# Alternating the solving product of one chunk with the inner product of the next in an RWKV-7 recurrence

## The chip, the cores and the metric

The kernel runs on one core of a Trainium2 chip. The metric is the time of one execution in device microseconds (us), here the median of several runs. A profile is one more execution, recorded by the hardware profiler; its times are counted from the first instruction.

## The reference, cut to what matters

The model is a decoder trunk of two layers over 16 meta tokens and 256 tokens of width 2048: RWKV-7 time mixing, a squared-ReLU MLP, gated linear attention, a second MLP, all in float32. The change lies in the first layer. With 32 heads of 64, the reference runs its recurrence token by token:

```python
    def step(S, inp):
        r_t, w_t, k_t, v_t, a_t, b_t = inp
        sa = jnp.einsum('bhvk,bhk->bhv', S, a_t)
        S = S * w_t[:, :, None, :] + sa[..., None] * b_t[:, :, None, :] + v_t[..., None] * k_t[:, :, None, :]
        y = jnp.einsum('bhvk,bhk->bhv', S, r_t)
        return S, y
```

Each head's output `y` is then normalised over its 64 values, gets a bonus term, is multiplied by a gate and goes through the output matrix `w_o`.

## The kernel before, in words

Activations lie transposed, features on the partitions, as 16 tiles of 128 x 272 tokens. Large products are made of float32r products: weights and operands are split into a high and a low part, and three products replace one (`mm3`, L156 to L162). A weight of 128 x 1024 is loaded by a DMA of SyncE's queue (SP) into one of three buffers `raw` (L131), cast to `hi` on ScalarE (ACT, L137) and subtracted to `lo` on VectorE (DVE, L138); of `hi` and `lo` there are two buffers.

The recurrence works on chunks of 64 tokens (five per head, the last with 16) and on 16 heads at a time: two groups `g`, each with chunks `c` from 0 to 4 (L892 to L970). Within a chunk the token-by-token update becomes a triangular system per head. Its inverse is worked out beforehand on DVE (`invert`, L539: 30 steps of two instructions, for two chunks and all 16 heads of a group at once). The system reaches DVE through DRAM (`scores`, L512, stores it with DMAs), and the inverse goes back through DRAM into the tile `AM` (L562). Because only 32 x 32 blocks are inverted so, `merge` (L636) completes a 64 x 64 inverse on TensorE in two rounds (L645, L655) of 32 x 32 products. There are four inversions and merges: number 2g for chunks 0 and 1 of group g, number 2g + 1 for the rest.

A chunk then has these steps on TensorE, each of 16 small float32 products, one per head, if nothing else is said. `AM` holds a chunk's matrices: partitions 0 to 63 multiply the values `v`, partitions 64 to 127 hold the inverse.

- `centre` (L663): eight products that transpose the values of a chunk and take out their mean; ACT copies them to the upper half of `uv` (L674, two copies). For the short chunk 4 GpSimd (POOL) clears `uv` first (L672).
- `inner` (L686): the values by the lower half of `AM`, into a bank of `pu`, called `ra`.
- `state` (L702): the state `S` by the keys, added to `ra` (L719), and by the receptances, into `pry` (L717): 32 products, taken in turn for the first part. Then `sides` (L695) negates `ra` into `rs` with two ACT instructions (L699). For chunk 0, which has no state, `inner` calls `sides` itself.
- `solve` (L722): the inverse by `rs`, into another bank of `pu` (L728); ACT copies the result to the second half of `uv` (L731).
- `carry` (L734): one product that puts `S` into a bank of `pu`, and `learn` (L739): keys by `uv` added to it; DVE scales the sum to the new `S` (L744).
- `emit` (L746): `uv` by the receptance half of `AM` (L752), the chunk's output; ACT copies it out (L754).
- `keys` (L676): eight transposes for the next chunk's `learn`.

The tag `pu` has two PSUM banks, given out in turn; `pm` (for centre and half of keys) has one.

The order on TensorE in this part is written out by hand (`manual_schedule`, L886). The other engines' queues get theirs from the scheduler, ordered by priority, weights far ahead. Between the small products stand *filling* units of large products: `R(n)` (L867) runs `n` units, `until(n)` (L872) runs on to unit number n, and a unit is three products of one weight column block. The 512 units are, in this order (L844): the value projection (units 0 to 255), then the output matrix in parts: 0 (256 to 287), 1 (288 to 319), A (320 to 383), 2 (384 to 447), 3 (448 to 511). An output part can begin only when the heads of its part are normalised (`norm`, L756) and split (L788). Eight units use up one weight. `some(it, n)` runs n steps of a generator, mostly of `invert`, whose instructions go to DVE. `GAPS` (L47) gives the units after `state` and after `solve` for each chunk; `MARK` (L49) gives the unit numbers that have to be reached before the four merges. In group 1 the scores for inversion 3 come first, with `R(3)` between them (L899).

At the very start, while the first activations are squared and summed, TensorE runs products without use (L361, L379) on a tile of ones, so that it is not idle.

Of the kernel before, what the change touches and what calls it, by code (L numbers as in the profile page):

```python
# [43 lines left out]

GAPS = [(4, 2), (4, 2), (4, 2), (4, 3), (5, 5)]  # L47

MARK = [120, 170, 244, 302]  # L49

OUTQ = [0, 1, 4, 5]
OUTA = [4, 5, 6, 7, 12, 13, 14, 15]
# [2 lines left out]
class Kern:  # L55
# [235 lines left out]
    def rwkv(self, done):  # L291
        nc, tc, ap = self.nc, self.tc, self.ap
# [23 lines left out]
        idle = self.pu()  # L316
# [42 lines left out]
        with tc.manual_schedule(engines={ENG.PE, ENG.DVE, ENG.Activation}):  # L359
            for _ in range(3):  # L360
                nc.tensor.matmul(idle, warm[:, :128], warm[:, :512], start=True, stop=True)  # L361
            for i in range(8):
                sq, h = self.t(ep, [P, 2, T], "x", KT), d[:, 2 * i : 2 * i + 2]
# [6 lines left out]
                for k in range(2 if i in (2, 5, 7) else 1):  # L370
                    nc.tensor.matmul(ss, warm[:, :128], sq[:, k], start=i == 0, stop=i == 7 and k == 1)
            w = warm.bitcast(F32R)
            v = w[:, :512]
            for x in (v.rearrange("p (a t) -> p t a", a=4), v.rearrange("p (a t c) -> p t a c", a=2, c=2),
                      v.rearrange("p (b a t) -> p b t a", a=2, t=16), v.rearrange("p (t a) -> p a t", a=2)):
                o = idle.rearrange("p (t a) -> p t a", a=x.shape[2]) if len(x.shape) == 3 else idle.rearrange(
                    "p (t a c) -> p t a c", a=x.shape[2], c=x.shape[3])
                for _ in range(3):
                    nc.tensor.matmul(o, w[:, :128], x, start=True, stop=True)  # L379
            om0 = self.one_minus(ep, "mix0")  # L380
            self.omka = self.one_minus(self.cp, "k_a")
            rstd = self.rstd_from(ep, ss, T, 1.0 / D, NORM_EPS, "kn", 2)
# [16 lines left out]
            def weight(kt):  # L399
                if kt:  # L400
                    raw = self.t(self.wp, [P, 1024], "raw", self.raw_bufs)
                    nc.sync.dma_start(raw, ap["w_r0"][kt])
                else:
                    raw = raw0
                return [raw] + [self.t(self.wp, [P, 1024], n, self.hi_bufs, F32R) for n in ("hi", "lo")]
# [9 lines left out]
            for kt in range(KT):  # L415
                w = weight(kt)
# [14 lines left out]
                p = parts.pop(0)  # L431
# [132 lines left out]
        for f in range(KT):  # L564
# [45 lines left out]
            if f == 13:  # L610
                inv = invert(0)
# [51 lines left out]
        def centre(g, c):  # L663
            full, n, nr = geom(c)[:3]
            pv = self.pm()
            for p in range(4):
                for e in range(2):
                    nc.tensor.matmul(pv[64 * e : 64 * e + nr, p * P : (p + 1) * P], hres[:, 8 * g + 4 * e + p, c * C : c * C + nr],
                                     self.cent, start=True, stop=True)
            x = uvs[g, c] = self.t(kp, [P, 16, 64], "uv", 2)  # L670
            if not full:
                nc.gpsimd.memset(x[0 : 2 * n], 0.0)  # L672
            for e in range(2):
                nc.scalar.copy(x[:nr, 8 * e : 8 * e + 8], pv[64 * e : 64 * e + nr].rearrange("p (h v) -> p h v", h=8))  # L674
# [11 lines left out]
        def inner(g, c):  # L686
            full, n, nr, am, lo, up, at = geom(c)
            uv = uvs[g, c]
            ra = ras[g, c] = bank(self.pu())
            for h in range(16):  # L690
                nc.tensor.matmul(ra[at[h % 2], h // 2], am[:n, h, :n], uv[:n, h], start=h < 2, stop=c == 0 and h > 13)
            if c == 0:
                sides(g, c)

# [7 lines left out]
        def state(g, c):  # L702
            full, n, nr, am, lo, up, at = geom(c)
            AR, ra = ARs[c > 1], ras[g, c]
            o = 128 * (c % 2) if full else 256
            ry = rys[g, c] = bank(self.pry())
            pq = [(p, q) for p in range(8) for q in range(2)]
            turns = [(*x, 0) for x in pq]
            outs = [(p, 1 - q, 1) for p, q in pq]
            if full:  # L710
                for i in range(7):
                    turns.insert(1 + 3 * i, outs.pop(0))

            for p, q, i in turns + outs:
                rows = slice(64 * q, 64 * q + 64)
                if i:
                    nc.tensor.matmul(ry[rows, p, :nr], sb[rows, p], AR[rows, p, o + n : o + n + nr], start=p == 0, stop=False)  # L717
                else:
                    nc.tensor.matmul(ra[at[q], p], AR[rows, p, o : o + n], sb[rows, p], start=False, stop=p == 7)  # L719
            sides(g, c)  # L720

        def solve(g, c):  # L722
            full, n, nr, am, lo, up, at = geom(c)
            uv, rs, pu = uvs[g, c], ras[g, c, "rs"], bank(self.pu())
            nu = n if full else 16
            for h in range(16):
                o = n * (1 - h % 2)
                nc.tensor.matmul(pu[o : o + nu, h // 2], am[up, h, :nu], rs[up, h], start=True, stop=True)  # L728
            for q in range(2):
                o = n * (1 - q)  # L730
                nc.scalar.copy(uv[n : n + nu, q::2], pu[o : o + nu])  # L731


        def carry(g, c):  # L734
            pS = pSs[g, c] = bank(self.pu())
            if c:
                nc.tensor.matmul(pS, self.ident, sb, start=True, stop=False)
# [129 lines left out]
        def R(n):  # L867
            for _ in range(n):
                if next(work, work) is not work:
                    ran[0] += 1  # L870

        def until(n):  # L872
            R(n - ran[0])

        def some(it, n):
            for _ in range(n):
                next(it, None)
# [8 lines left out]
        with tc.manual_schedule(engines={mybir.EngineType.PE}):  # L886
            R(43)
            for c, e in units1:
                some(inv, 5)
                R(13)  # L890
                scores(1, c, e)
            for g in range(2):  # L892
                last = nothing
                if g:

                    last = norm(0)
                    some(last, 1)
                    for c, e in units1:
                        R(3)  # L899
                        some(last, 1)  # L900
                        scores(3, c, e)
                    last = norm(1)
                until(MARK[2 * g])
                some(inv, 99)
                m = merge(2 * g)
                next(m)
                some(last, 1)
                R(4)
                next(m)
                inv = invert(2 * g + 1)  # L910
                some(inv, 3)
                until(128 + 128 * g)
                centre(g, 0)
                some(last, 1)
                R(2)
                keys(g, 0)
                some(last, 1)
                R(2)
                inner(g, 0)
                for _ in last:  # L920
                    R(4)
                    some(inv, 3)
                R(2)
                for c in range(5):
                    if c == 2:
                        R(8)
                        some(inv, 99)
                        if g == 0:
                            scores(2, 0, 0)
                        until(MARK[2 * g + 1])  # L930
                        m = merge(2 * g + 1)
                        next(m)
                        R(4)
                        next(m)
                        R(4)
                    if c:
                        state(g, c)
                    if g == 0 and c == 1:
                        fetch(2, ARs, ard)
                    if g == 0 and c == 2:  # L940
                        scores(2, 0, 1)
                    R(GAPS[c][0])
                    some(inv, 8)
                    solve(g, c)
                    if c < 4:
                        centre(g, c + 1)
                    if g == 0 and c == 2:
                        scores(2, 1, 0)
                    if c < 4:
                        carry(g, c)  # L950
                    R(GAPS[c][1])
                    some(inv, 8)

                    if c < 4:
                        learn(g, c)
                        inner(g, c + 1)
                    if g == 0 and c == 2:
                        scores(2, 1, 1)
                        inv = invert(2)
                    emit(g, c)  # L960
                    if c < 3:
                        keys(g, c + 1)
                    if g == 0:
                        if c == 0:
                            fetch(2, BKs, bkd)
                        if c == 2:
                            fetch(3, BKs, bkd)
                        if c == 4:
                            fetch(3, ARs, ard)
                    some(inv, 5)  # L970
            for g in (2, 3):
                for _ in norm(g):
                    R(2 * g)
# [298 lines left out]
```

## Time and profile before

| what | us |
|---|---|
| median of 3 runs | 2416.78 (2416.39 to 2419.48) |
| the profiled execution | 2421.71 |
| its span, first to last instruction | 2419.9 |
| TensorE busy in the span | 2371.1 |
| DVE busy | 1640.0 |
| ACT busy | 1242.5 |
| recurrence, about | 320 to 545 |

In a profile, PE is TensorE's products, PEld its weight loads, and `L728` line 728 of the kernel. A float32 product counts as two instructions. A row of the timeline reads: start, duration, engine, line, operation, output <- inputs, the tile and operand sizes, the count; in brackets the idle time before it and what ended that. A row of waits reads: total in us, number, longest. A product's duration contains its way through the array, so that rows overlap; what a group costs is seen from the start of one group to the start of the next.

### The profile page before, as it was taken

The numbers are of one execution on the slowest core, as the hardware profiler recorded it, in microseconds if no ns is written. First come the engines' busy times: TensorE is split into PE (matmuls) and PEld (weight loads), VectorE is DVE, ScalarE is ACT, GpSimd is POOL, SyncE is SP. The second block draws the span as 40 slices with busy tenths as digits, with TensorE's granted clock in tenths as the row PEclk, the third lists the DMA queues.
The fourth block names the chain that finished last, engine by engine and source line by source line (L and its number), as shares of the span: only waits on it lengthen the run. The fifth ranks groups of instructions, "written<-read, shape, count | busy, mean of one in ns | idle before, by whom it ended". The sixth has DMA issues, their size and how long they took to land. (4 is left out here: it accounts for less than half of the span.)

```text
span 2419.9 us, 47169 instructions
## 1 busy us (share of the span) xinstructions
PE 2371.1 (98%) x19262; PEld 2235.7 (92%) x19262; DVE 1640.0 (68%) x2748; ACT 1242.5 (51%) x1951; POOL 6.6 (0%) x20
## 2 busy tenths in 40 slices
PE   9999999899999999999999999999999999999998
PEld 8888888889999999999999999998999999999997
DVE  8777986858655555555556788778766666666666
ACT  6366544455555445345345555555555545445444
POOL 0000000000000000000000000000000000000000
PEclk9999999999999999999999999999999999999999
DMA  5578864524555555555555544445566666666665
GB/s 210 167 234 293 249 192 136 151 80 164 172 188 190 192 191 188 189 192 191 187 190 191 190 159 162 159 158 182 195 202 202 202 200 200 201 201 201 201 202 171
DMA packets 160729, 455.29 MB, mean 188 GB/s; under 512 B 34112, under 2 KB 50624, under 8 KB 160512
## 3 DMA queue, kind: packets, MB, share of 16 engines
q1 hardware_dynamic: 160512, 452.27, 57.4%
q8 instruction: 151, 2.47, 0.4%
q14 instruction: 66, 0.54, 0.1%
HBM read 433.86 MB, written 18.35 MB: 187 GB/s over the span
## 5 line engine op out<-in xcount | busy, mean ns | idle before, releaser
L137 ACT CAST hi<-raw 128x1024 fp32r<-128x1024 f32 (+1 forms) x818 | 794.3, 978 | 950.4 <-PE pj L161 524.8
L138 DVE TENSOR_TENSOR lo<-raw,hi 128x1024 fp32r<-128x1024 f32 (+1 forms) x818 | 926.2, 1139 | 512.1 <-ACT hi L137 503.5
L160 PE MATMUL pj<-x,hi 128*128 128x272 f32 x2240 | 640.7, 286 | 4.4 <-DVE hres L293 2.8
L162 PE MATMUL pj<-x,lo 128*128 128x272 f32 x2240 | 631.4, 282 | 5.8 <-DVE lo L138 5.6
L161 PE MATMUL pj<-x,hi 128*128 128x272 f32 x2240 | 628.2, 280 | 0.0
L189 PE MATMUL pj<-x,hi 128*128 128x512 f32 x1664 | 550.5, 384 | 3.8 <-ACT hi L137 3.0
L190 PE MATMUL pj<-x,lo 128*128 128x256 f32 x1664 | 457.0, 275 | 1.6 <-DVE lo L138 1.5
L160 PEld LDWEIGHTS pj<-x,hi 128*128 128x128 f32 x2240 | 424.3, 189 | 12.6 <-issue 4.7
L162 PEld LDWEIGHTS pj<-x,lo 128*128 128x128 f32 x2240 | 424.3, 189 | 10.7 <-DVE lo L138 9.6
L161 PEld LDWEIGHTS pj<-x,hi 128*128 128x128 f32 x2240 | 424.5, 190 | 3.2 <-issue 1.4
L189 PEld LDWEIGHTS pj<-x,hi 128*128 128x128 f32 x1664 | 315.3, 189 | 48.0 <-ACT hi L137 3.7
L189 PE MATMUL pj<-h,hi 128*128 128x512 f32 x1008 | 330.3, 382 | 0.0
L190 PEld LDWEIGHTS pj<-x,lo 128*128 128x128 f32 x1664 | 320.1, 192 | 4.6 <-DVE lo L138 4.1
L160 PE MATMUL pj<-h,hi 128*128 128x272 f32 (+1 forms) x1040 | 290.1, 279 | 0.0
L161 PE MATMUL pj<-h,hi 128*128 128x272 f32 (+1 forms) x1040 | 290.1, 279 | 0.0
L162 PE MATMUL pj<-h,lo 128*128 128x272 f32 (+1 forms) x1040 | 290.1, 279 | 0.0
L190 PE MATMUL pj<-h,lo 128*128 128x256 f32 x1008 | 274.8, 273 | 0.0
L189 PEld LDWEIGHTS pj<-h,hi 128*128 128x128 f32 x1008 | 190.5, 189 | 26.4
L160 PEld LDWEIGHTS pj<-h,hi 128*128 128x128 f32 x1040 | 196.6, 189 | 0.0
L161 PEld LDWEIGHTS pj<-h,hi 128*128 128x128 f32 x1040 | 196.6, 189 | 0.0
L162 PEld LDWEIGHTS pj<-h,lo 128*128 128x128 f32 x1040 | 196.6, 189 | 0.0
L190 PEld LDWEIGHTS pj<-h,lo 128*128 128x128 f32 x1008 | 193.5, 192 | 0.0
(268 smaller groups left out, 2115.4 us busy)
## 6 DMA issues: line engine op xcount, KB each, us to landing
raw<-mlp_w_d SPq DMA_DIRECT2D x512, 512.0 KB, 3.4
raw<-gla_in_d SPq DMA_DIRECT2D x98, 512.0 KB, 3.4
raw<-w_rkv_d SPq DMA_DIRECT2D x80, 512.0 KB, 4.0
raw<-gla_o_d SPq DMA_DIRECT2D x32, 512.0 KB, 3.4
raw<-rw_oQ_d SPq DMA_DIRECT2D x24, 512.0 KB, 3.3
raw<-w_r_d SPq DMA_DIRECT2D x16, 512.0 KB, 3.3
ard<-ar SPq DMA_DIRECT2D x16, 288.0 KB, 3.8
bkd<-bk SPq DMA_DIRECT2D x16, 288.0 KB, 3.9
```

The lines of the kernel that those rows point to most:

```text
L137: nc.scalar.copy(hi[:, h], raw[:, h])
L138: nc.vector.tensor_tensor(out=lo[:, h], in0=raw[:, h], in1=hi[:, h].bitcast(F32), op=ALU.subtract)
L160: nc.tensor.matmul(out, hi[:, ws], xh, start=first, stop=False)
L161: nc.tensor.matmul(out, hi[:, ws], xl, start=False, stop=False)
L162: nc.tensor.matmul(out, lo[:, ws], xh, start=False, stop=last)
L189: nc.tensor.matmul(wide, hi[:, ws], xt, start=kt == 0, stop=False)
L190: nc.tensor.matmul(one, lo[:, ws], xt[:, 0], start=False, stop=kt == nk - 1)
```

## The change

Six edits, all on the order of the instructions:

1. `inner` becomes a generator that stops after each product. `solve` gets a flag `beside`, and with it issues one product of the next chunk's `inner` after each of its own. It is set for chunks 0, 1 and 2. For chunk 3 `inner` of chunk 4 runs whole right after `solve`. Before, `inner` of the next chunk stood after `learn`.
2. `centre` of the next chunk moves from behind `solve` to ahead of the first filler.
3. `carry` moves from ahead of the second filler to behind it.
4. `GAPS` moves two units from ahead of `solve` to behind it, in chunks 0 to 3.
5. Two more units stand between the scores of inversion 3, and the marks for merges 1, 2 and 3 rise by 6, 22 and 26 units.
6. The last twelve products without use, in four access patterns, become thirteen in one.

```diff
-GAPS = [(4, 2), (4, 2), (4, 2), (4, 3), (5, 5)]
+GAPS = [(2, 4), (2, 4), (2, 4), (2, 5), (5, 5)]
-MARK = [120, 170, 244, 302]
+MARK = [120, 176, 266, 328]
...
-            v = w[:, :512]
-            for x in (v.rearrange("p (a t) -> p t a", a=4), v.rearrange("p (a t c) -> p t a c", a=2, c=2),
-                      v.rearrange("p (b a t) -> p b t a", a=2, t=16), v.rearrange("p (t a) -> p a t", a=2)):
...
-                for _ in range(3):
-                    nc.tensor.matmul(o, w[:, :128], x, start=True, stop=True)
+            x, o = self.weave(w[:, :512]), self.pairs(idle)
+            for _ in range(13):
+                nc.tensor.matmul(o, w[:, :128], x, start=True, stop=True)
...
             for h in range(16):
                 nc.tensor.matmul(ra[at[h % 2], h // 2], am[:n, h, :n], uv[:n, h], start=h < 2, stop=c == 0 and h > 13)
+                if h < 15:
+                    yield
...
-        def solve(g, c):
+        def solve(g, c, beside=False):
...
+            other = inner(g, c + 1) if beside else iter(())
             for h in range(16):
                 o = n * (1 - h % 2)
                 nc.tensor.matmul(pu[o : o + nu, h // 2], am[up, h, :nu], rs[up, h], start=True, stop=True)
+                next(other, None)
...
-                        R(3)
+                        R(5)
...
-                inner(g, 0)
+                some(inner(g, 0), 99)
...
+                    if c < 4:
+                        centre(g, c + 1)
...
                     R(GAPS[c][0])
                     some(inv, 8)
-                    solve(g, c)
-                    if c < 4:
-                        centre(g, c + 1)
+                    solve(g, c, c < 3)
+                    if c == 3:
+                        some(inner(g, 4), 99)
                     if g == 0 and c == 2:
                         scores(2, 1, 0)
+                    R(GAPS[c][1])
+                    some(inv, 8)
                     if c < 4:
                         carry(g, c)
-                    R(GAPS[c][1])
-                    some(inv, 8)
-
-                    if c < 4:
                         learn(g, c)
-                        inner(g, c + 1)
```

More of the change, by code (lines that the diff above doesn't have):

```diff
@@ L372, in rwkv @@
             w = warm.bitcast(F32R)
-            v = w[:, :512]
-            for x in (v.rearrange("p (a t) -> p t a", a=4), v.rearrange("p (a t c) -> p t a c", a=2, c=2),
-                      v.rearrange("p (b a t) -> p b t a", a=2, t=16), v.rearrange("p (t a) -> p a t", a=2)):
-                o = idle.rearrange("p (t a) -> p t a", a=x.shape[2]) if len(x.shape) == 3 else idle.rearrange(
-                    "p (t a c) -> p t a c", a=x.shape[2], c=x.shape[3])
-                for _ in range(3):
-                    nc.tensor.matmul(o, w[:, :128], x, start=True, stop=True)
+            x, o = self.weave(w[:, :512]), self.pairs(idle)
+            for _ in range(13):
+                nc.tensor.matmul(o, w[:, :128], x, start=True, stop=True)
             om0 = self.one_minus(ep, "mix0")
@@ L943, in rwkv @@
                     some(inv, 8)
-                    solve(g, c)
-                    if c < 4:
-                        centre(g, c + 1)
+                    solve(g, c, c < 3)
+                    if c == 3:
+                        some(inner(g, 4), 99)
                     if g == 0 and c == 2:
                         scores(2, 1, 0)
-                    if c < 4:
-                        carry(g, c)
                     R(GAPS[c][1])
@@ L954, in rwkv @@
                     if c < 4:
+                        carry(g, c)
                         learn(g, c)
-                        inner(g, c + 1)
                     if g == 0 and c == 2:
```

## The prediction

> **What bounds the kernel now.** I read the page first, then the summary of busy time by stretch for the recurrence (320 to 545 us), the list of waits of TensorE there, and last the timeline of single engines.
>
> ```profile
> span 2419.9 us, 47169 instructions
> PE 2371.1 (98%) x19262; PEld 2235.7 (92%) x19262; DVE 1640.0 (68%) x2748; ACT 1242.5 (51%) x1951; POOL 6.6 (0%) x20
> ```
>
> TensorE is busy for 98% of the span. So only TensorE work that becomes shorter, a TensorE wait that goes, or a better clock can pay. The change touches the start and the recurrence; there are few waits there:
>
> ```profile
> PE pt L655 <- DMA AM<-invd: 4.4, 2, 3.3
> PE pt L522 <- DVE AM L293: 2.3, 5, 1.0
> ```
>
> In the busy time by stretch, the first number after the stretch is its length, the next TensorE's busy time, and the number after POOL's the granted clock:
>
> ```profile
> 378.90:382.30 3.40, 2.27 (x72) 2.12 (x73) 0.00 (x0) 1.35 (x4) 0.00 (x0) 1.00 0.90 215
> 382.30:385.80 3.50, 3.50 (x70) 3.25 (x68) 1.65 (x3) 2.00 (x5) 0.00 (x0) 0.51 0.24 32
> ...
> 450.60:454.00 3.40, 1.05 (x10) 0.77 (x8) 2.09 (x4) 2.07 (x5) 0.27 (x1) 1.00 0.74 174
> 454.00:460.80 6.80, 5.84 (x79) 5.78 (x80) 0.82 (x4) 1.46 (x4) 0.16 (x1) 0.50 0.85 209
> 460.80:545.00 84.20, 83.04 (x1411) 74.67 (x1411) 51.58 (x125) 48.49 (x96) 0.94 (x1) 1.00 0.33 99
> ```
>
> The two waits of merge (L655) for the inverse's DMA lie in the first and third of these stretches, and after each the clock is half: for 3.5 us, and for 6.8 us.
>
> **The change, part by part.** The times of one chunk (group 0, chunk 1) carry most of the sum:
>
> ```profile
> 354.98 0.27 PE L719 MATMUL pu<-S,AR 64*64 64x64 f32 x1
> ...
> 355.90 0.22 PE L719 MATMUL pu<-S,AR 64*64 64x64 f32 x1
> 355.91 0.22 PE L717 MATMUL pry<-AR,S 64*64 64x64 f32 x1
> ...
> 356.47 0.38 PE L160 MATMUL pj<-x,hi 128*128 128x272 f32 x1
> ...
> 356.92 0.28 PE L160 MATMUL pj<-x,hi 128*128 128x272 f32 x1
> ...
> 358.06 1.15 PE L728 MATMUL pu<-rs,AM 64*64 64x64 f32 x32
> 359.14 1.09 PE L668 MATMUL pm<-cst,hres 128*64 128x128 f32 x16
> 360.16 1.13 PE L737 MATMUL pu<-S,cst 128*128 128x512 f32 x2
> ...
> 362.99 1.15 PE L691 MATMUL pu<-uv,AM 64*64 64x64 f32 x32
> ```
>
> *1. Solve and the next inner alternately, six times (two groups, chunks 0 to 2).* Now solve takes 1.08 us from its start to that of the next group (358.06 to 359.14), and inner, busy for the same 1.15, as long: 16 products each, two records a product. Within a group a product takes (1.15 - 0.22) / 16 = 0.058 us; some 0.15 is the change to the next group. Alternated, they read different halves of the rows (solve 64 to 127, inner 0 to 63) and write two banks. The nearest row is state, whose 32 products also go to two banks, partly in turn: 354.98 to 356.47, 1.49 us, where 32 x 0.058 + 0.15 = 2.01 would be serial. The middle rows show why: a product to pu and one to pry start 0.01 us apart. I take 1.49: 2.16 - 1.49 = 0.67 saved, six times **-4.0 us**. Ends: if all pairs run side by side, 16 x 0.058 + 0.21 = 1.14, so -6.1; if none does, 2.01, so -0.9. The low end has a row of its own: the scores alternate row halves and two banks as well, and are as slow as solve:
>
> ```profile
> 328.91 1.15 PE L522 MATMUL pt<-AR,BK 64*64 64x64 f32 x32
> ```
>
> The Trainium skill, TensorEngine Tiling (Array Packing), Key Properties, says of the tiles that they "operate independently: Different tiles can execute LdWeights and Matmul in parallel". By that the term would be the -6.1; the state row agrees in part, the scores row does not.
>
> *2. Centre moved ahead of solve, carry behind the second filler.* Centre's eight products (1.02 us) and carry's one (0.56) cost the same at either place. What moves with centre is ACT's work:
>
> ```profile
> 356.24 1.21 ACT L699 ACTIVATE rs<-pu 64x512 f32<-64x512 f32 x2 [0.46 <-PE pu L719]
> 358.05 1.14 ACT L137 CAST hi<-raw 128x512 fp32r<-128x512 f32 x2 [0.61 <-PE pj L161]
> 359.50 1.18 ACT L731 COPY uv<-pu 64x512 f32<-64x512 f32 x2
> 360.70 1.19 ACT L674 COPY uv<-pm 64x512 f32<-64x512 f32 x2
> ```
>
> The cover of sides (rs, 1.21 us) was four filler units; a unit is three products, 0.35 us (356.92 to 358.06 is three units and the turn to solve). It becomes centre (1.02) and two units (0.70), which is longer, so solve does not wait for sides. New is that the alternated inner needs centre's two uv copies. They start behind sides, at 357.5, and end at 358.7. TensorE arrives at 356.5 + 1.02 + 0.70 + 0.1 = 358.3 and needs the second copy eight pairs later. So the wait is about 0.1 at best, and 1.1 if the weight cast (1.14) gets in front of the copies. Queued behind a waiting inner product are all later TensorE products, the solve products among them. A weight is cast every eight units and a chunk has six; I let the cast hit one group of the six: +1.2, ends 0 and 6.6. Solve's own copies (1.18) then have four units (1.4) as cover before learn.
>
> Chunk 3 is not alternated, but its inner leaves the place between learn and state, where it hid the state's scaling on DVE:
>
> ```profile
> 408.20 0.68 DVE L293 TENSOR_TENSOR S<-pu,WC 128x512 f32<-128x512 f32 x1
> ```
>
> ```profile
> 409.29 1.08 PE L719 MATMUL pu<-S,AR 64*32 64x64 f32 x32
> ```
>
> State would now start 1.0 us sooner, at 408.3, and wait until 408.9; in chunks 0 to 2 keys still covers it. Twice 0.4: +0.8, ends 0 and 1.4. Chunk 4's POOL memset moves ahead with centre; it waits only for the emit two chunks back. New waits together **+2.0 us**.
>
> *3. Scores: five units instead of three between them.* TensorE waits there for DVE's masking of the scores before: five waits, 2.3 us. Ten units more give each 0.70 us, which takes all of four waits and most of the longest. DVE works in order and the inverse is in its queue, so I take **-1.5**, ends 0 and -2.3.
>
> *4. Merge of group 1 (mark 244 to 266).*
>
> ```profile
> 454.96 1.91 PE L655 MATMUL pt<-AM,rs 32*32 32x32 f32 x62 [3.28 <-DMA AM<-invd]
> ```
>
> Counted through the loops, the filler between the start of inverse 2 and this product grows from 64 to 80 units: 16 x 0.35 = 5.6 us. Less 1.5 of scores' waits, TensorE comes 4.1 us later against the inverse, and the wait is 3.28. The inverse's own chain ends in loads from SP's queue:
>
> ```profile
> 453.53 0.35 SPq L131 DMA_DIRECT2D raw<-rw_oQ_d x1
> 453.94 0.43 SPq L562 DMA_DIRECT2D AM<-invd x1
> ```
>
> Sixteen units bring two weights, each with one load on SP, two casts on ACT and two subtractions on DVE, but scores and normalisation are spread over a longer time, so DVE has no more to do before the inverse is done. The loads of the inverse stand in SP's queue behind weight loads (453.53 before 453.94), and two more weights go past them now. I take the wait as gone, -3.3, and with it the half clock: from 454.96 to 460.8 TensorE ran at half, 5.8 / 2 = -2.9. Together **-6.2**, ends 0 and -6.2.
>
> *5. Merge in group 0 (mark 170 to 176).* Of merge's 4.4 us of waits 1.1 are left for this one. Six units are 2.1 us, but two alternated groups before it bring TensorE 1.3 earlier, less waits of 0.4: net it comes 1.2 later. With full pairs (2.0 for 1.3) it comes 0.5 later. I take **-0.6** and no change of clock, ends 0 and -2.9 (1.1, and half of 3.5).
>
> *6. Warm-up: 13 products in one pattern for 12 in four.*
>
> ```profile
> 11.63 4.22 PE L379 MATMUL pu<-ar 128*128 128x512 f32 x12
> 15.67 0.42 PE L444 MATMUL pj<-x,hi 128*128 128x272 f32 x2
> ```
>
> ```profile
> 15.22 0.21 PEld L444 LDWEIGHTS pj<-x,hi 128*128 128x128 f32 x1 [0.24 <-ACT x L329]
> ```
>
> ```profile
> 1899.74 0.38 PE L189 MATMUL pj<-x,hi 128*128 128x512 f32 x1
> 1899.96 0.27 PE L190 MATMUL pj<-x,lo 128*128 128x256 f32 x1
> ```
>
> The twelve take 4.04 us and hold the first real product to 15.67, though its operand is there at 15.22. The nearest row for the new pattern, a product with 512 columns over alternating halves, takes 0.22 from start to start: 13 x 0.22 = 2.9. So at most 0.45 goes; I take **-0.2**. If the pattern were as slow as the last of the twelve (15.22 to 15.67), 13 x 0.45 would end 1.8 later.
>
> *7. Filling.* The units are the same in number: the last filling runs to 448 in both, so the 26 moved ahead of the last merge leave the end, where TensorE is full of the same products. I cost it at nothing. If products of layer output 2 (unit 384, now within the last normalisation) come before their operand is split, up to +1.5.
>
> Sum: -4.0 + 2.0 - 1.5 - 6.2 - 0.6 - 0.2 = -10.5. The profiled execution took 2421.7 us (1.8 around its span of 2419.9): 2411.2. The median is 2416.8, 4.9 less than it; carried over, **2406.3 us**.
>
> **The rivals.**
>
> *A: the alternation runs serially*, as the scores do, so the change doesn't do what it says. For it: the scores row. Against it: the state rows. The term is -0.9 instead of -4.0; TensorE comes later to merge 1, so 0.5 more of that wait goes: 2408.9 us.
>
> *B: merge 2 still waits*, for half its time, since the inverse's loads are queued behind more weights on SP, and the clock still falls: -1.6 instead of -6.2, 2410.9 us.
>
> *C: ACT casts a weight ahead of centre's copies every time.* Six waits of 1.1 and two of 0.7, 8.0 for 2.0: 2412.3 us. For it: the cast at 358.05 stands just there. Against: it was ready only when a weight was used up, once in eight units.
>
> *D, the other side: C and the clock.* The first stretch above holds a wait of 1.1 us and 2.27 busy of 3.40, and the next 3.5 us had half the clock. Six waits of 1.1 in the alternated groups, each followed by such a stretch, cost 6 x 1.7 = 10.2 on top of C: 2422.5 us. It decides from the third such stretch on (C leaves -4.5). Against it: the stretch from 460.8 kept clock 1.00 through many small products.
>
> The Trainium skill, TensorE: Matmul & The Clock Gate, HAM oscillation, warns of idle gaps over about 3.4 us only; by that D would stay at C's time. The trace does not agree: 1.1 us was enough once, though beside the 32x32 products.
>
> **How the numbers follow.** The forecast has 0.52, A 0.17, B 0.13, C 0.10, D 0.08. All best ends together (-6.1, 0, -2.3, -6.2, -2.9, -0.45) give 2398.8, but are not expected at once; A and C together give 2414.9. The range from 2400 to 2416 leaves out D and the extremes. About 0.2%, 4.8 us, is what a measurement of this kernel can tell from no change, so faster means under 2412.0: nearly all of the forecast and A, half of B, a little of C: 0.70. Within 0.2% is the rest of these, 0.20; slower is D and mishaps of its kind, 0.10.
>
> **What the profile after would show.** Step 1: L728 and L691 start 0.01 us apart, and the group takes 1.1 to 1.5 us; 2.0 is A. Step 2: TensorE's waits at L691 for uv of L674, none in sum over 2 us; at L719 for S in chunk 4. Steps 3 to 5: the L522 and L655 waits small, the clock 1.00 around the later merge. Step 6: L444 at about 15.3. The prediction is wrong if the clock falls elsewhere in the recurrence, or if the waits of L655 come back with the new marks.

## The result: 0.4% slower, and the profile after

| | median us (range, runs) | profiled execution | its span |
|---|---|---|---|
| before | 2419.01 (2416.39 to 2421.48, 6) | 2421.71 | 2419.9 |
| after | 2427.88 (2423.47 to 2434.41, 6) | 2423.47 | 2421.7 |

The ratio is 1.0041, with a 95% interval of 1.003 to 1.0051: slower by 8.9 us, where I forecast 10.5 us faster. The two profiled executions are only 1.8 us apart, since the one of before is longer than all six of its row and the one of after is the shortest of its six. So the traces show where the time goes, and the medians how much.

From the page of after, the head and the group of L160:

```profile
span 2421.7 us, 47169 instructions
PE 2362.8 (98%) x19263; PEld 2227.4 (92%) x19263; DVE 1640.1 (68%) x2748; ACT 1243.4 (51%) x1951; POOL 6.6 (0%) x20
...
L160 PE MATMUL pj<-x,hi 128*128 128x272 f32 x2240 | 639.5, 285 | 15.1 <-DVE hres L293 14.4
```

TensorE is busy for 8.3 us less than before (2371.1), and yet the kernel takes longer. The third row says why: 15.1 us of idle time ahead of L160, 14.4 of it on a DVE result in `hres`. L160 is filler; before, this group had 4.4. The waits of TensorE from 320 to 545 us (total, number, longest):

```profile
PE pj L160 <- DVE hres L293: 11.5, 2, 9.6
PE pj L162 <- DVE lo L138: 2.9, 2, 1.8
PE pu L717 <- DVE S L293: 2.4, 2, 2.0
PE pt L518 <- DVE AM L293: 2.0, 3, 1.3
```

Merge (L651 now) is no longer in the list: its waits of 4.4 us are gone. In their place stands one wait of 9.6 us in the filler ahead of merge 2. The timeline of TensorE there, only the rows of that wait and of the merge's two rounds:

```profile
460.94 0.57 PE L160 MATMUL pj<-x,hi 128*128 128x272 f32 x1 [9.64 <-DVE hres L293]
...
462.56 1.92 PE L641 MATMUL pt<-sysA,AM 32*32 32x32 f32 x64
...
467.43 1.76 PE L651 MATMUL pt<-AM,rs 32*32 32x32 f32 x58
```

The product waits for a bank of `pj`, and DVE frees it by adding the residual to it. DVE's timeline, its split of the outputs and that addition:

```profile
445.58 1.49 DVE L293 TENSOR_TENSOR x<-hres,x 128x272 fp32r<-128x272 f32 x4
...
460.35 0.82 DVE L293 TENSOR_TENSOR hres<-pj,hres 128x272 f32<-128x272 f32 x2 [7.19 <-DMA hres<-hT_d]
```

The split reads `hres` for the last time at 447.1; from then on the residual may be loaded into it. SP's queue:

```profile
445.34 3.31 SPq L131 DMA_DIRECT2D raw<-rw_oQ_d  x2
448.76 0.37 SPq L558 DMA_DIRECT2D AM<-invd  x1
450.14 0.33 SPq L131 DMA_DIRECT2D raw<-rw_oQ_d  x1
450.52 0.42 SPq L558 DMA_DIRECT2D AM<-invd  x1
453.19 0.33 SPq L131 DMA_DIRECT2D raw<-rw_oQ_d  x1
453.56 0.96 SPq L558 DMA_DIRECT2D AM<-invd  x2
454.57 1.91 SPq L831 DMA_DIRECT2D hres<-hT_d  x4
```

The residual (L831) stands behind weight loads and the inverse's pieces, and is issued at 454.57, 7.5 us after it could have been. It lands at 460.3. The weight loads ahead of it wait themselves: of SP's waits from 440 to 465 us the largest is that of L131 for `lo` (L138), 4.7 us in two, that is for a buffer `raw` to come free.

The same stretch by time; the columns are as in the prediction, the DMA engines' share is the next to last number:

```profile
445.00:451.30 6.30, 6.29 (x52) 5.88 (x51) 4.92 (x11) 2.96 (x7) 0.00 (x0) 1.00 0.58 185
451.30:460.90 9.60, 0.00 (x0) 0.00 (x0) 1.85 (x4) 1.05 (x2) 0.00 (x0) 0.69 0.90 215
460.90:475.40 14.50, 14.46 (x174) 12.84 (x175) 5.55 (x19) 4.99 (x12) 1.10 (x2) 0.50 0.01 4
475.40:545.00 69.60, 66.75 (x1249) 59.62 (x1247) 44.02 (x103) 39.41 (x76) 0.95 (x1) 1.00 0.38 111
```

Behind the wait, TensorE works through 14.5 us at half its clock, which costs another 7.2 us. Before, the stretch behind merge 2's wait had 6.8 us at half clock.

The clock accounts for about the whole loss. The mean granted clock of after's six runs is 0.9917; that of 31 runs of before (those beside E1 to E4) is 0.9968. Each run's time multiplied by its clock has a median of 2407.8 after and 2409.5 before (the clock is given to three digits, so one run is uncertain by 1.2 us); what is missing to the full time, the loss at half clock, grew from about 8 to about 20 us. This product counts a wait at half clock only half: in the trace of after 6.0 of the 9.6 us of waiting are at half clock, so some 3 of the 20 us belong to the wait. What TensorE has to do, waits among it, is then about as long as before.

### The profile page after: what moved, and what is told of

It is laid out like the page before. It is cut to its first block, busy times and chain, and to the rows that moved or that the text cites. A ratio compares the mean times of both kernels' runs of the same rounds, so it can differ in the third digit from the quotient of the medians.

```text
span 2421.7 us, 47169 instructions
## 1 busy us (share of the span) xinstructions
PE 2362.8 (98%) x19263; PEld 2227.4 (92%) x19263; DVE 1640.1 (68%) x2748; ACT 1243.4 (51%) x1951; POOL 6.6 (0%) x20
## 5 line engine op out<-in xcount | busy, mean ns | idle before, releaser
L138 DVE TENSOR_TENSOR lo<-raw,hi 128x1024 fp32r<-128x1024 f32 (+1 forms) x818 | 926.3, 1139 | 516.4 <-ACT hi L137 507.8
L160 PE MATMUL pj<-x,hi 128*128 128x272 f32 x2240 | 639.5, 285 | 15.1 <-DVE hres L293 14.4
L160 PEld LDWEIGHTS pj<-x,hi 128*128 128x128 f32 x2240 | 424.3, 189 | 23.4 <-issue 15.9
L160 PE MATMUL pj<-h,hi 128*128 128x272 f32 (+1 forms) x1040 | 290.1, 279 | 0.0
L160 PEld LDWEIGHTS pj<-h,hi 128*128 128x128 f32 x1040 | 196.6, 189 | 0.0
```

What stands on the lines that cost most here:

```text
L138: nc.vector.tensor_tensor(out=lo[:, h], in0=raw[:, h], in1=hi[:, h].bitcast(F32), op=ALU.subtract)
L160: nc.tensor.matmul(out, hi[:, ws], xh, start=first, stop=False)
```

## The experiments

"Before" here is the kernel before, run on the same chip; its median was 2415.9 to 2418.1. Clock is the mean granted clock of the runs. Each kernel has one trace, and the half clock differs between its executions (those of E16 took 2404.87 to 2414.53 us, at clocks from 0.999 to 0.996), so the stretches below show what happens in one execution, not its mean.

| kernel | median us (range, runs) | ratio to before [95%] | clock |
|---|---|---|---|
| E14 before, mark 266 | 2423.84 (2421.32 to 2428.33, 11) | 1.0025 [1.0017, 1.0034] | 0.9953 |
| E3 before, all filling edits | 2423.91 (2421.38 to 2431.79, 8) | 1.0029 [1.0017, 1.0042] | 0.9942 |
| E4 after, old filling and warm-up | 2416.98 (2413.40 to 2419.55, 11) | 0.9996 [0.9987, 1.0004] | 0.9961 |
| E1 after, parts on `r` first | 2420.74 (2414.77 to 2423.79, 11) | 1.0009 [1.0000, 1.0019] | 0.9950 |
| E2 after, mark 250 | 2420.70 (2416.64 to 2429.68, 12) | 1.0017 [1.0006, 1.0028] | 0.9938 |
| E7 after, residual on POOL's queue | 2421.27 (2415.03 to 2426.55, 12) | 1.0009 [0.9998, 1.0020] | 0.9951 |
| E8 E7, inverse steps issued later | 2420.71 (2418.09 to 2425.28, 11) | 1.0012 [1.0003, 1.0020] | 0.9947 |
| E9 E7, no alternation | 2422.25 (2417.05 to 2428.74, 12) | 1.0020 [1.0009, 1.0030] | 0.9942 |
| E10 E8, inverse's pieces on POOL too | 2412.63 (2406.35 to 2418.36, 12) | 0.9979 [0.9969, 0.9988] | 0.9958 |
| E11 before, both loads on POOL | 2411.12 (2408.57 to 2412.51, 6) | 0.9969 [0.9957, 0.9980] | 0.9980 |
| E12 E10, no alternation | 2414.12 (2409.08 to 2419.65, 11) | 0.9990 [0.9979, 1.0001] | 0.9956 |
| E13 E10, S covered | 2408.46 (2403.25 to 2413.25, 6) | 0.9955 [0.9939, 0.9972] | 0.9977 |
| E15 E4, both loads on POOL | 2408.91 (2407.05 to 2412.07, 7) | 0.9969 [0.9958, 0.9980] | 0.9971 |
| E16 E15, no alternation | 2408.94 (2404.87 to 2414.53, 9) | 0.9969 [0.9957, 0.9980] | 0.9978 |

The theory (W): the new mark lets output part 0 begin ahead of merge 2, its residual is late, and the wait takes the clock down. The rivals: the new order itself costs the clock (O), or the gains come out but are given back elsewhere (G).

### Does the filling alone make the loss?

**E14**, one number in the kernel before:

```diff
-MARK = [120, 170, 244, 302]
+MARK = [120, 170, 266, 302]
```

> The kernel before with one number changed: the mark of merge 2 is 266 instead of 244. Theory W (output part 0 stands ahead of merge 2 and waits for its residual): a wait of L160 for hres of 6 to 10 us, no wait of L655 over 1.5 there, at least 10 us at half clock behind it, 2420 to 2426 us. Rival P (the prediction's step 4: the wait of 3.3 for the inverse's pieces goes and nothing takes its place): 2411 to 2415 us.

Measured: 2423.84, 6.7 us slower. Its waits, and the stretch at half clock:

```profile
PE pj L160 <- DVE hres L293: 8.3, 1, 8.3
PE pt L522 <- DVE AM L293: 2.3, 5, 1.0
PE pt L655 <- DMA AM<-invd: 1.8, 1, 1.8
```

```profile
457.00:467.40 10.40, 6.14 (x82) 5.86 (x82) 2.10 (x8) 1.46 (x4) 1.10 (x2) 0.51 0.36 103
```

This is theory W. One number brings the wait (8.3 us), the half clock and most of the loss (6.7 of 8.9 us). Units 256 to 259 fill one bank of `pj` and 260 to 263 the other; unit 264 needs the first again. By this count a mark of 266 asks for it ahead of merge 2; and since four more units stand between the merge's two rounds, only a mark up to 260 would keep it behind them. No run tried a mark between 250 and 266. (The L655 wait of 1.8 us is that of merge 1, at 378.8; the clock stays full behind it.)

**E3**, all edits to the filling on the kernel before:

```diff
-MARK = [120, 170, 244, 302]
+MARK = [120, 176, 266, 328]
...
-                        R(3)
+                        R(5)
```

> The kernel before, with the filling moved alone: the new marks and five units between the scores, nothing else. W: the wait at unit 264 and the half clock are there, and nothing of the alternation's gain: 2428 to 2438 us. O: as the kernel before or a little faster, 2412 to 2420.

Measured: 2423.91, the same as E14, with a wait of 7.5 us for `hres` and 17.1 us at half clock beside it. The signs are those of W, but the time lies below its range (2428 to 2438) and above that of O. The other marks and the scores' spacing change nothing that can be seen beside it.

**E4**, the other half: the kernel after with the old marks, `R(3)` and the old warm-up.

```diff
-MARK = [120, 176, 266, 328]
+MARK = [120, 170, 244, 302]
...
-                        R(5)
+                        R(3)
```

> The changed kernel with the old marks, three units between the scores and the old warm-up: alternation, centre, carry and gaps alone. W: no wait at unit 264; the alternation saves about 1 us in each of six places: 2409 to 2415 us. O: slower than before, 2423 to 2430.

Measured: 2416.98, no different from before. So the order costs nothing, which speaks against O, but brings nothing either, where W said 2409 to 2415. Merge's two waits are as before (4.3 us in two). In this trace other waits of TensorE grew: for `lo` from 1.0 to 2.9 us, for `r` from 0.7 to 1.3, and there are new ones of 1.0 for centre's copy `uv` and of 0.9 for `S`, 4.4 us together, against six groups shorter by some 1.07.

### What if the wait is taken away?

**E1** puts the output parts that add into `r`, not `hres`, first; their loads are issued between 425 and 441 us. **E2** keeps merge 2 ahead of output part 0.

```diff
-OUTQ = [0, 1, 4, 5]
+OUTQ = [4, 5, 0, 1]
```

```diff
-MARK = [120, 176, 266, 328]
+MARK = [120, 176, 250, 328]
```

> The changed kernel, with output part 0 (and 1) taken in the order of columns 8-15 first (OUTQ 4, 5, 0, 1), so that the first additions use residuals that are loaded early. Theory W (the filling moved ahead of merge 2 starts output part 0 before its residual is loaded: a wait of 9.6 us at unit 264 and about 14.4 us at half clock after it, 7.2): the wait goes, the half clock with it, 10 to 17 us under the changed kernel, 2411 to 2418 us. Rival O (the new order around solve, with its own waits and small products, brings the clock down): the same as the changed kernel, 2425 to 2431.

> The changed kernel with the mark of merge 2 at 250 instead of 266, so that no unit of output part 0 runs ahead of it. W: the wait at unit 264 shrinks from 9.6 to 0 to 3 us, but a wait of 2 to 4 us for the inverse comes back at L651: 2413 to 2420 us. O: 2425 to 2431.

Measured: 2420.74 and 2420.70. The 9.6 us are gone in both, and the ratio falls from 1.0041 to 1.0009 and 1.0017, 6 to 8 us; but neither is faster than before, and both times lie between the ranges of W and O. W said that the half clock would go with the wait; it did not. E1's trace has four stretches of it, 20.5 us in all, each begun at or just behind a wait: for `S` (408.2), for a score's mask (442.4), at merge 2 (462.9) and for `r` (507.2). The waits of E1:

```profile
PE pt L651 <- DMA AM<-invd: 4.3, 1, 4.3
PE pj L160 <- DVE r L293: 2.9, 1, 2.9
PE pj L162 <- DVE lo L138: 2.9, 2, 1.8
PE pu L717 <- DVE S L293: 2.8, 1, 2.8
```

TensorE now comes to merge 2 before the inverse's pieces, and waits 4.3 us there, longer than before (3.3), in spite of the 80 units that I had counted as enough. The pieces pass SP's queue as well. The residual was the latest of two late loads.

**E7** leaves all as in after and loads the residual through POOL's queue, which is nearly empty (6.6 us busy).

```diff
                 if s == 0:
-                    nc.sync.dma_start(loc[f], ap["hT"][:, f])
+                    nc.gpsimd.dma_start(loc[f], ap["hT"][:, f])
```

> The kernel after, with the residual of the output parts (hres<-hT_d) loaded on POOL's queue instead of SP's. Theory W (the filler ahead of merge 2 waits for a residual that is late because it stands in SP's queue behind weight loads and the inverse's pieces; the 9.6 us of waiting and the 20.5 us at half clock that follow are the loss): the wait of L160 for hres goes below 1 us, TensorE reaches merge 2 some 9 us sooner and there waits 3 to 4.5 us for the inverse's pieces, as in the version with the parts reordered; half clock around it at most 7 us; 2414 to 2420 us. Rival P (POOL's own issue of a load is slow, or the load is late for what it must itself wait for): a wait of more than 4 us for hres stays, 2422 to 2430. Rival O (the new order with its short groups holds the clock down, whatever waits): the half clock between 400 and 480 us stays at 15 us or more, 2420 to 2426.

Measured: 2421.27, 1.3 above W's range and inside O's. The residual is no longer late: the split reads `hres` from 451.52 on, and the first residual is issued at 452.25.

```profile
451.52 1.49 DVE L293 TENSOR_TENSOR x<-hres,x 128x272 fp32r<-128x272 f32 x4
```

```profile
452.25 2.12 POOL L831 DMA_DIRECT2D hres<-hT_d  x4 [8.56 <-DVE x L293]
```

The wait for it ahead of merge 2 is gone, as W said. But the first two waits of TensorE are

```profile
PE pt L651 <- DMA AM<-invd: 4.9, 2, 4.6
PE pj L160 <- DVE hres L293: 2.9, 1, 2.9
```

(the second at 507.8, long after merge 2, where after has one of 1.9), and the longest of its three stretches at half clock lies elsewhere, ahead of them:

```profile
400.00:410.20 10.20, 8.14 (x186) 6.99 (x187) 5.51 (x18) 3.61 (x8) 0.15 (x1) 1.00 0.63 200
410.20:420.40 10.20, 10.20 (x91) 9.71 (x88) 7.13 (x18) 3.38 (x6) 0.00 (x0) 0.50 0.54 180
```

The first of these stretches holds the one wait for `S` (2.1 us); 10.2 us at half clock follow, and 6.8 more at merge 2: 17 us between 400 and 480 us, where W allowed 7 and O asked for 15. So W is right on the residual and wrong on the clock. O's reason, the short groups themselves, isn't needed for it: E9 below has none of them and 20.5 us at half clock, and E15, with the change's order on the old marks, has none from 320 to 545 us. What the order did bring is the longer wait for `S`.

**E10** takes the inverse's pieces off SP's queue too (and has the later inverse steps of E8, below):

```diff
-                    nc.sync.dma_start(x, invd[b][rows].rearrange("h s t -> s h t"))
+                    nc.gpsimd.dma_start(x, invd[b][rows].rearrange("h s t -> s h t"))
```

> As the kernel with the late inverse steps, and the inverse's pieces (AM<-invd) are loaded on POOL's queue too, so that they stand behind no weight load. Theory W: the waits of L651 go below 1 us in sum, the clock stays full around merge 2, 2408 to 2413 us: faster than both kernels. Rival M (the pieces were late for the inverse itself, not for the queue): the wait at merge 2 stays above 3 us, 2412 to 2418. Rival O: no wait, but half clock for 10 us or more between 400 and 480 us, 2414 to 2420.

Measured: 2412.63, the upper end of W, faster than both kernels. Half clock is left in two pieces of 3.4 us, at 408.9 and 439.6, behind waits for `S` and a score's mask. Two of its waits:

```profile
PE pj L160 <- DVE hres L293: 1.5, 1, 1.5
...
PE pt L651 <- DMA AM<-invd: 0.7, 1, 0.7
```

Rival M falls: merge 2 has no wait left to speak of, so the pieces were late for the queue.

**E11**: is it the change that then pays? The kernel before, with the same two lines changed:

> The kernel before, with the residual and the inverse's pieces loaded on POOL's queue, and nothing of the change. Theory Q (what the change could win in the merges is a matter of the queue alone): the waits of L655 fall from 4.4 to under 1.5 us, the half clock beside them goes, and the time is 2409 to 2413, no more than 1.5 above the changed kernel with both loads on POOL's queue. Rival D (the change pays once the queue is free, by its shorter groups): 2414 to 2417 us, at least 2 above that kernel.

Measured: 2411.12, theory Q. The waits of merge fall from 4.4 to 0.7, no stretch of the recurrence is at half clock, and the change adds nothing that can be told (E10: 2412.63).

```profile
PE pt L655 <- DMA AM<-invd: 0.7, 1, 0.7
```

```profile
435.00:470.00 35.00, 33.19 (x406) 30.59 (x406) 30.34 (x79) 20.54 (x47) 5.89 (x10) 1.00 0.62 171
```

What I had hoped to win in the merges by filling is won by the queue, without filling.

### The wait for S

**E8**: E7, with the steps of inverse 2 put behind the scaling of `S` in chunk 3 of group 0.

```diff
                     R(GAPS[c][0])
-                    some(inv, 8)
+                    if g or c != 3:
+                        some(inv, 8)
...
                     R(GAPS[c][1])
-                    some(inv, 8)
+                    late = g == 0 and c == 3
+                    if not late:
+                        some(inv, 8)
...
                         learn(g, c)
+                    if late:
+                        some(inv, 16)
...
-                    some(inv, 5)
+                    some(inv, 1 if g == 0 and c == 2 else 5)
```

> As the last, and in group 0 the DVE steps of inverse 2 that stood ahead of the scaling of S in chunk 3 are put behind it. Theory W: the wait of L717 for S falls from 2 to 2.8 us to under 0.8, the half clock that follows it in some runs goes with it; inverse 2 starts about as late as before, since it waits for its load anyway; 1.5 to 4 us less than the kernel with the residual on POOL's queue. Rival L (inverse 2 gets later by what S gains, and merge 2 waits for it): the same time as that kernel within 1 us, with the wait of L651 longer by 2 us or more.

Measured: 2420.71, the same as E7 ("the last" in the expectation). But the edit didn't do what it was for. DVE's queue is ordered by the scheduler, and the timeline of DVE shows inverse steps still ahead of `S`:

```profile
404.77 0.18 DVE L293 TENSOR_TENSOR upd<-sysA 64x30 f32<-64x30 f32 x1 [3.99 <-DMA sysA<-sysd]
...
407.11 0.68 DVE L293 TENSOR_TENSOR S<-pu,WC 128x512 f32<-128x512 f32 x1
```

DVE idles 3.99 us for the inverse's load, then runs nine instructions of the inverse, and only then scales `S`, whose sum is ready soon after 404. TensorE waits 2.7 us. Neither theory was tested by this run.

**E13** is E10 with that wait covered:

```diff
-MARK = [120, 176, 266, 328]
+MARK = [120, 176, 272, 328]
-OUTQ = [0, 1, 4, 5]
+OUTQ = [4, 5, 0, 1]
...
-                    if c == 3:
+                    if c == 3 and g:
                         some(inner(g, 4), 99)
...
                     emit(g, c)
+                    if c == 3 and not g:
+                        some(inner(g, 4), 99)
+                        R(6)
```

> The changed kernel with both loads on POOL's queue; in chunk 3 of group 0 inner(4) and six units are issued between emit and the next state, where TensorE waits up to 3.2 us for the scaling of S; the mark of merge 2 goes from 266 to 272, and the output parts on r go first. Theory S (that wait and its half clock are a loss of their own): no wait of L717 over 0.5 us, full clock from 400 to 430 us, 2407 to 2411 us. Rival G (merge 2 or the residual is bound by the inverse's and the norm's chains, which start no earlier): the waits of L651 and L160 grow by 2 to 3 us, and the time is within 1.5 us of the kernel without this edit, 2411 to 2414.

Measured: 2408.46, inside theory S, with no half clock in the recurrence. But the wait for `S` isn't under 0.5 us, it is 2.2 us in two from 400 us on, the longest 1.4; and the interval touches that of E10 (0.9969 to 0.9972 lies in both). That it beats before and after is shown; what each of its three edits brings isn't, nor that it beats E11, whose interval overlaps its own too.

### Does alternation reach the end?

**E9**, **E12** and **E16** are E7, E10 and E15 with each inner product whole behind solve:

```diff
-                    solve(g, c, c < 3)
-                    if c == 3:
-                        some(inner(g, 4), 99)
+                    solve(g, c)
+                    if c < 4:
+                        some(inner(g, c + 1), 99)
```

> As the kernel with the residual on POOL's queue, but every inner product is issued whole behind solve instead of alternately; all else stays. Theory W (each of the six alternated groups is 1.07 us shorter, and that reaches the end): 5 to 7 us more than the kernel with the residual on POOL's queue. Rival G (the gain is given back at the next wait for an inverse's pieces, for the scaling of S or for a score's mask): 0 to 3 us more, with these waits shorter here by as much.

> The changed kernel with both loads on POOL's queue and the late inverse steps, but every inner product is issued whole behind solve. The traces of the pair with the residual alone on that queue gave 1.84 us for the two groups one behind the other and 1.14 alternated. Theory W (with no wait for an inverse's pieces to give it back to, six times 0.70 reaches the end): 2415 to 2418 us, 3 to 5 more than the alternated one. Rival G (the gain is given back at the split of a weight on DVE and at the scaling of S): within 1.5 us of the alternated one.

**E15** is E4 with the two lines of POOL's queue.

> The order of the change alone (old marks, old units between the scores, old warm-up) with both loads on POOL's queue, so that neither the residual nor the inverse's pieces hold the merges. Theory W (the alternation's gain reaches the end when nothing gives it back and the clock stays full): 2406 to 2409 us, 2 to 5 below the kernel before with both loads on that queue (2411). Rival G (the gain is given back at the scaling of S, at a weight's split and at merge 2, which TensorE reaches earlier than its inverse is done): 2409.5 to 2413.

> As the last, but every inner product is issued whole behind solve. Theory W: 3 to 5 us more than the alternated one (six times 0.70). Rival G: within 1.5 us of it.

Measured, alternated and whole: 2421.27 and 2422.25, 2412.63 and 2414.12, 2408.91 and 2408.94. The timeline of TensorE in E9, from solve to the filler behind inner (354.13 to 355.97):

```profile
354.13 0.97 PE L727 MATMUL pu<-rs,AM 64*64 64x64 f32 x26
354.89 0.27 PE L687 MATMUL pu<-uv,AM 64*64 64x64 f32 x2
...
355.97 0.38 PE L160 MATMUL pj<-x,hi 128*128 128x272 f32 x1
```

One behind the other the two take 1.84 us: the first inner products start while solve runs. In E7 they take 1.14, so alternation itself is worth 0.70 a group, 4.2 in six. In the pair E7 and E9 the time from the start of merge 0 to that of merge 1 is nevertheless the same, 43.9 us (333.46 to 377.33 and 330.37 to 374.28): the filler between waits for a weight's split on DVE, in E7

```profile
371.41 0.38 PE L162 MATMUL pj<-x,lo 128*128 128x272 f32 x1 [1.83 <-DVE lo L138]
```

and in E9

```profile
368.36 0.38 PE L162 MATMUL pj<-x,lo 128*128 128x272 f32 x1 [0.44 <-DVE lo L138]
```

1.4 us, all that two groups gained. That is rival G, in this stretch of this pair; in the other pairs the same stretch is shorter with alternation, by 1.3 us (E10 and E12) and 0.6 (E15 and E16). Over the whole kernel the differences of the medians are 1.0, 1.5 and 0.0 us; the ratios to before differ by 0.11%, 0.11% and nothing, with intervals 0.1% to either side. Six times 0.70 did not come out in any pair. Whether 0 or 2 us reach the end stays open.

E15 lies in W's range in microseconds, 2.2 under E11. But before was 1.3 us faster beside E15 than beside E11, and the two ratios are the same, 0.9969: the order as a whole brings nothing that the medians can tell. The two traces do differ from the start of merge 0 to that of merge 3, E15 first:

```profile
333.35:492.75 159.40, 152.27 (x2548) 135.43 (x2547) 124.60 (x314) 87.14 (x176) 16.78 (x28) 1.00 0.51 149
```

```profile
334.67:497.25 162.58, 156.94 (x2548) 140.73 (x2547) 124.12 (x314) 87.26 (x176) 16.78 (x28) 1.00 0.50 145
```

At full clock the same 2548 instructions of TensorE take 3.2 us less in the new order. That is one execution of each; it points to a gain, and doesn't show one.

## Why the prediction was wrong, step by step

- **Step 1 (-4.0), mis-sized in the group, and not a gain at the end.** After, the pairs run side by side, at the better end that I gave:

```profile
488.35 0.27 PE L727 MATMUL pu<-rs,AM 64*64 64x64 f32 x1
488.35 0.27 PE L687 MATMUL pu<-uv,AM 64*64 64x64 f32 x1
...
489.44 0.38 PE L160 MATMUL pj<-x,hi 128*128 128x272 f32 x1
```

  1.09 us for both, where 2.16 stood before: 1.07 less, 6.4 in six. The value from the state row was too cautious. Rival A is out. Here the Trainium skill's sentence on independent tiles (TensorEngine Tiling (Array Packing), Key Properties) agrees with the trace. But I let the gain run to the end, and the experiments didn't find more than 2 us of it there.
- **Step 2 (+2.0), the sum right by chance.** No wait for centre's copies was left in after (I took 1.2; rival C is out). In E4 and E15, with the old marks, there is one, of 1.0 and 0.7 us: one group of six, as I took it. The wait for `S` is 2.4 instead of 0.8, nearly all of it in group 0:

```profile
407.79 1.08 PE L717 MATMUL pu<-S,AR 64*32 64x64 f32 x32 [2.05 <-DVE S L293]
```

  I had priced DVE's 0.68 for `S` and left out what is queued ahead of it: steps of inverse 2 that wait for their load. Before, the row of `S` at 408.20 had the same queue ahead of it, and inner and emit hid it.
- **Step 3 (-1.5), mis-sized:** 2.3 to 2.0, so -0.3. Ten units more hardly shortened these waits; that DVE's own order sets when the mask is done is my reading, not shown by a run.
- **Step 4 (-6.2) failed, by step 7.** "I take the wait as gone, -3.3, and with it the half clock." The wait at L651 went, and a longer one stood ahead of it: 9.6 for 3.3 us, and 14.5 us of work at half clock for 5.8. E14 shows it with the mark alone. And the wait for the pieces is only hidden: without the residual it is 4.2 to 4.6 us (E1, E2, E7). That they stand behind weight loads was written there, and rival B had its cause; I then judged by the inverse's steps, not by the queue.
- **Step 5 (-0.6), about right:** merge 1's wait of 1.1 and the 3.5 us of half clock behind it are gone in after, while the wait for a weight's `lo` grew from 1.0 to 2.9.
- **Step 6 (-0.2), not told apart:** the 51st L160 product starts at 52.1 before and at 51.6 after, but with the old warm-up also at 51.8 (E4) and 51.5 (E15).
- **Step 7 (0) failed.** "I cost it at nothing." The units are the same in number, but not in kind. Units from 256 on are output products: they need split operands, and in part 0 each column block issues a residual load on SP and frees its bank only when that load has landed. I looked at unit 384, not at 256, which the new mark passes by ten. The view of DMA issues of before, from 430 to 465 us, had the price:

```profile
hres<-hT_d SPq DMA_DIRECT2D x4, 136.0 KB, 5.2
```

  5.2 us from issue to landing, and behind weight loads at that; the first bank is wanted again after eight units, which are 2.8 us.
- **Rival D** named the right penalty at the wrong place: waits of some 2 us take the clock down, at `S` and at merge 2, not in the alternated groups. I gave it 0.08.

## What to carry to other kernels

Where filler is moved, list for every unit what it reads, what it loads and what frees its bank: a unit of another kind brings its own DMA, and a DMA in an ordered queue is as late as the loads ahead of it. Before covering a wait for a transfer with work, see in which queue the transfer stands, and what the loads ahead of it wait for; here, two lines that moved it to an empty queue gave 6 us (E11), and the cover gave a loss. And follow a gain to the next thing that TensorE waits for: in one pair of runs, 1.4 us of two shorter groups came back there as a wait for a weight.

## What the runs showed of the hardware

- **A short wait can cost more than itself through the clock.** In E8, a wait of 2.75 us for `S` is followed by

```profile
409.80:413.00 3.20, 3.20 (x19) 3.16 (x18) 1.93 (x6) 1.22 (x3) 0.00 (x0) 0.50 0.53 120
```

  and in E7 one of 2.1 us by 10.2 us at half clock. The Trainium skill (TensorE: Matmul & The Clock Gate, HAM oscillation) gives idle gaps of over about 3.4 us as the limit; the runs disagree. Between 320 and 545 us half clock came in pieces of 3.41 us (E8) and multiples: 6.83 (before), 10.24 (E7, E14), 17.07 (E3), 20.48 (after). Not every wait brings it: E13, with waits of up to 1.9 us, and E15 kept full clock from 320 to 545 us, and at merge 1 a wait of 1.1 us in before was followed by 3.4 us at half clock, one of 1.8 us in E14 by none. What decides it stays open.
- **Products of different tiles run side by side over the seam of two groups, too** (E9, 354.89: inner starts while solve has products left), if they read different row halves and write different banks. The scores, with row halves and two banks as well, stayed as slow as before (1.15 us for 16 products of chunk 4 in both traces); why is open.
